# Up-projection of a gated MLP: seven products of half-size blocks in place of eight, with the inner features kept in DRAM

## The chip, the cores and the metric

The kernel runs on one core of a Trainium2 chip. The metric is the device time of one execution in microseconds, the median of three runs. TensorE is called PE here, VectorE DVE, ScalarE ACT, GpSimd POOL, and SyncE, which issues most of the loads, SP.

## What is computed

One decoder block on a sequence of 1024 tokens with 1024 features, in float32: attention of two kinds (stick-breaking and multi-head latent, MLA), an output projection, and a gated MLP with a causal convolution of width 3 over the tokens, all with RMSNorm and residuals. The part that matters here:

```
h = rms_norm(x, g_pre_ffn)
u = causal_depthwise_conv(h @ w_up, conv_w, conv_b)      # 1024 x 1024 times 1024 x 5632
gate, val = split(u, 2)                                  # 2816 features each
f = (gelu(gate, approximate=True) * val) @ w_down        # 2816 x 1024
x = x + rms_norm(f, g_post_ffn)
e = p @ w_ple
g = sigmoid(rms_norm(x, g_ple_gate) @ w_ple_gate + b_ple_gate)
x = x + rms_norm(g * e, g_post_ple)
```

## The kernel before, in words

Every matrix product is made from two float32r parts of each operand, a high and a low one (`split`, L90 to L97: ACT casts the high part, DVE or POOL subtracts to get the low part), and three of the four part products are added in PSUM. So one block of 128 x 128 weights times 512 tokens costs three matmuls with 512 columns, each of form 128*128 by 128x512.

Tokens go in two halves of 512 (`th` 0 and 1). After the attention the order is: output projection and norms of half 1 (`out_proj_sb`, `out_proj_mla`, L757 to L808), with the up-projection of half 0 (`ffn_up(0)`) filled in between; the rest of `ffn_up(0)`; `ffn_down(0)`; `ffn_up(1)`; `ffn_down(1)`; and the gate stage at the end.

`ffn_up` (L870) walks over 22 chunks `c` of 128 inner features. For a chunk it makes the gate's 128 rows (v=0) and the value's (v=1): 8 weight blocks times 3 matmuls for each, 48 matmuls in all (L895, L897, L901). The weights come through `split_w` (L107), 256 KB at a time, by the SP queue. The convolution reads PSUM: ACT multiplies by one tap and adds the bias (L913), DVE adds the other taps (L915, L917), and the two tokens at the seam between the halves go through the tile `halo` (L920 to L924). Gelu is ACT's (L938), the product with the value part DVE's (L939). The 22 feature tiles `f` stay in SBUF. `ffn_down` splits them and multiplies by `w_down` in 2 column halves x 22 chunks x 12 matmuls (L116 to L118).

What sets the order: the code is written as generators, and a `Fill` object steps the filler (here `ffn_up(0)`) by a credit at each yield of the main one; `WO_RATE` is the credit per yield of the output projection. A scheduler then orders the instructions of each engine by priority. Each engine runs its queue in that order, and so a waiting instruction holds all behind it. In `out_proj_mla(1)` a chain of steps ends the half: squares (L783), reciprocal roots (L125 to L135), scaling on DVE (L788), the residual's addition on POOL (L793), squares again, scaling (L800), and transposes on PE (L804), from which ACT and DVE make `h2`, the operand of the up-projection.

Of the kernel before, what the change touches and what calls it, by code (L numbers as in the profile page):

```python
# [38 lines left out]
WO_RATE = (1.0, 1.5)  # L39
AHEAD = 0.9  # L40
EMB_RATE = 1.0

LATER = (500, 0, 0, 2000)
# [6 lines left out]
def tile_hybrid_block(ctx: ExitStack, tc: tile.TileContext, a: dict, out: bass.AP):  # L50
# [13 lines left out]
    v_dram = dram.tile([P, NT, H], F32, name="v_dram")  # L64

# [213 lines left out]
    with tc.tile_pool(name="pre", bufs=1) as pre, \  # L279
# [27 lines left out]
        halo = const.tile([P, 2 * NCH, 2], F32, name="halo")  # L307
# [410 lines left out]
    def group_rstd(c0, ts):  # L718
# [3 lines left out]
        for j, t in enumerate(ts):  # L722
            src = o_tile(c0, t)
            sq = tmp().rearrange("p (c t) -> p c t", c=4)
            s_ = [sh.tile([P, P], dt, tag=f"s{i}", name=nm("s"))
                  for i, dt in enumerate((F32, F32R, F32R))]
            ps = bank()
            group_ssq(src, sq, s_, ps)
            dve.tensor_copy(ssm[:, j:j + 1], ps[:, 0:1])
            yield True  # L730
# [36 lines left out]
    def out_proj_mla(th, rows, h2):  # L767
# [8 lines left out]
        yield from group_product(4, ts, consume)  # L776
        hd_ = (slice(0, H), slice(H, D))
# [19 lines left out]
        for j in range(4):  # L797
            for k4, h_ in enumerate(hd_):
# [6 lines left out]
                d = [z[:, k4 * 4:k4 * 4 + 4, j * P:(j + 1) * P] for z in h2]  # L805
                split(d[0], d[1], ps.rearrange("p (k t) -> p k t", k=4))
                yield "chain"
# [33 lines left out]
    def embed_late():  # L841
        yield from embed(1, [sh.tile([P, H], F32R, tag=x, name=nm("pe"), bufs=b)
                             for x, b in (("y0", 1), ("y1", 1), ("raw", 1), ("t2", 6))])
# [12 lines left out]
    def f_tile(c):  # L856

        def two(p_, tag, bufs, first):
            if (c - first) % 2 == 0:
                f_tile.t = p_.tile([P, 2, H], F32, tag=tag, name=nm("f"), bufs=bufs)  # L860
            return f_tile.t[:, (c - first) % 2]

        if c < 8:
            return two(sh, "s4", 4, 0)
        if c < 14:
            return sh.tile([P, H], F32, tag="t2", name=nm("f"), bufs=6)
        if c < 18:
            return now["f"](c)
        return two(sh, "gb", 2, 18)

    def ffn_up(th, h2, f):
        nh, nl = h2
        todo = [(v * NCH + c, k4) for c in range(NCH) for v in range(2) for k4 in range(2)]
        ready = []

        def ahead(n):
            while len(ready) < n and todo:
                ci, k4 = todo.pop(0)
                ready.append(split_w(a["w_up"][ci, :, k4 * 4:k4 * 4 + 4, :], 512, None,
                                     now.get("light")))  # L880

        for c in range(NCH):
            ys = []
            while c >= 14 and "f" not in now or c >= 18 and "last" not in now:
                yield "wait"
            fc = f_tile(c)
            for v in range(2):
                ci = v * NCH + c
                ps = bank()
                for k4 in range(2):  # L890
                    ahead(3)
                    wh, wl = ready.pop(0)
                    for k in range(4):
                        kk = k4 * 4 + k
                        pe.matmul(ps, wh[:, k * P:(k + 1) * P], nh[:, kk], start=kk == 0,  # L895
                                  stop=False)
                        pe.matmul(ps, wh[:, k * P:(k + 1) * P], nl[:, kk], start=False, stop=False)  # L897
                    yield
                    for k in range(4):
                        kk = k4 * 4 + k  # L900
                        pe.matmul(ps, wl[:, k * P:(k + 1) * P], nh[:, kk], start=False,  # L901
                                  stop=kk == NK - 1)
                    if k4 == 0:
                        yield
                y = sh.tile([P, H], F32, tag=f"y{v}", name=nm("y"))
                if now.get("light"):
                    raw = sh.tile([P, H], F32, tag="raw", name=nm("raw"), bufs=1)
                    act.copy(raw, ps)
                    ps = raw
                    pool.tensor_scalar(y, ps, conv_w[:, ci, 2:3], conv_b[:, ci:ci + 1], ALU.mult,  # L910
                                       ALU.add)
                else:
                    act.activation(y, ps, AF.Identity, bias=conv_b[:, ci:ci + 1],  # L913
                                   scale=conv_w[:, ci, 2:3])
                dve.scalar_tensor_tensor(y[:, 1:], ps[:, :H - 1], conv_w[:, ci, 1:2], y[:, 1:],  # L915
                                         ALU.mult, ALU.add)
                dve.scalar_tensor_tensor(y[:, 2:], ps[:, :H - 2], conv_w[:, ci, 0:1], y[:, 2:],  # L917
                                         ALU.mult, ALU.add)
                if th == 0:
                    act.copy(halo[:, ci], ps[:, H - 2:])  # L920
                else:
                    dve.scalar_tensor_tensor(y[:, 0:1], halo[:, ci, 1:2], conv_w[:, ci, 1:2],
                                             y[:, 0:1], ALU.mult, ALU.add)
# [424 lines left out]
```

## Time and profile before

| | us |
|---|---|
| median of three runs | 1577.84 (1576.06 to 1579.86) |
| the profiled execution: its own time | 1584.88 |
| its span, from the first to the last instruction | 1583.1 |
| PE busy | 1479.8 |
| DVE busy | 1075.7 |
| ACT busy | 841.2 |
| POOL busy | 279.1 |

The profile has one execution. Groups of instructions are given by line, engine, operation and tile, with their number, busy time and mean duration; a second view gives busy time by stretches of the span; a third lists instructions in order of time. A matmul's duration overlaps with the next one's, since PE is pipelined: the distance from start to start is what one costs when PE never waits.

### The profile page before, as it was taken

How to read it: one execution, taken by the hardware profiler on the slowest of the kernel's cores; microseconds unless marked ns; L12 is line 12 of the kernel's file. 1: busy time of each engine (PE TensorE's matmuls, PEld its weight loads, DVE VectorE, ACT ScalarE, POOL GpSimd, SP SyncE). 2: the span in 40 equal slices, each digit the busy share in tenths (PEclk: the TensorE clock that was granted, in tenths of full speed). 3: DMA queues.
4: the chain of work that ended last, by engine and by line, in shares of the span. 5: the costliest groups of instructions: out<-in, count | busy, mean ns of one | idle time of the engine just before them, and what ended most of it. 6: DMA issues, size and time to landing. Idle time of an engine off the chain costs nothing. (4 is left out here: it accounts for less than half of the span.)

```text
span 1583.1 us, 20827 instructions
## 1 busy us (share of the span) xinstructions
PE 1479.8 (93%) x7032; PEld 1212.8 (77%) x7032; DVE 1075.7 (68%) x2021; ACT 841.2 (53%) x1649; POOL 279.1 (18%) x319
## 2 busy tenths in 40 slices
PE   4998998987899898899999999999999999999996
PEld 3977886865678676777888788888888888888875
DVE  4559477899777767866658855445976656444798
ACT  5356465677777675655544544444544444444542
POOL 7106300002243334241114000000000000000033
PEclk9999999999899899999999999999999999999998
DMA  6031310113444424234435532223432222233354
GB/s 197 22 100 41 106 35 14 47 53 126 143 139 148 130 90 157 67 110 145 150 117 191 169 103 88 99 93 99 152 122 94 93 94 96 92 95 97 127 178 168
DMA packets 109212, 173.78 MB, mean 110 GB/s; under 512 B 10913, under 2 KB 47681, under 8 KB 109105
## 3 DMA queue, kind: packets, MB, share of 16 engines
q1 hardware_dynamic: 100400, 142.71, 28.7%
q0 software_dynamic: 8704, 29.74, 5.1%
q8 instruction: 55, 0.90, 0.2%
q14 instruction: 53, 0.43, 0.1%
HBM read 142.26 MB, written 30.15 MB: 109 GB/s over the span
## 5 line engine op out<-in xcount | busy, mean ns | idle before, releaser
L94 DVE TENSOR_TENSOR wl<-ws,wh 128x512 fp32r<-128x512 f32 x281 | 203.9, 727 | 147.4 <-ACT wh L93 84.2
L93 ACT CAST wh<-ws 128x512 fp32r<-128x512 f32 x296 | 182.9, 620 | 219.6 <-PE mm L897 103.4
L897 PE MATMUL mm<-bh,wh 128*128 128x512 f32 x456 | 180.1, 395 | 0.0
L895 PE MATMUL mm<-bh,wh 128*128 128x512 f32 x456 | 180.1, 395 | 0.0
L94 DVE TENSOR_TENSOR fl<-f,fh 128x512 fp32r<-128x512 f32 x88 | 60.8, 692 | 117.9 <-PE mm L118 77.4
L94 DVE TENSOR_TENSOR tl<-tr,th 128x512 fp32r<-128x512 f32 x192 | 103.2, 550 | 45.3 <-ACT th L93 41.8
L901 PE MATMUL mm<-bh,wl 128*128 128x512 f32 x456 | 126.0, 396 | 0.0
L93 ACT CAST th<-tr 128x512 fp32r<-128x512 f32 x192 | 91.0, 485 | 59.6 <-PE tr L461 49.5
L93 ACT CAST fh<-f 128x512 fp32r<-128x512 f32 x88 | 54.6, 622 | 110.0 <-PE mm L117 84.4
L1166 POOL DMA_DIRECT2D x_dram<-fd x8 | 4.3, 538 | 616.9 <-DVE fd L1165 584.0
L461 PE MATMUL tr<-ident,w 128*128 128x128 f32 x576 | 102.6, 286 | 10.5 <-DVE tl L94 5.7
L895 PEld LDWEIGHTS mm<-bh,wh 128*128 128x128 f32 x456 | 85.9, 188 | 19.9
L897 PEld LDWEIGHTS mm<-bh,wh 128*128 128x128 f32 x456 | 85.9, 188 | 19.8
L901 PEld LDWEIGHTS mm<-bh,wl 128*128 128x128 f32 x456 | 85.6, 188 | 19.8
L649 DVE TENSOR_TENSOR_SCAN kc<-kc,one_f 128x128 f32<-128x128 f32 (+3 forms) x64 | 88.0, 1381 | 13.1 <-ACT kc L646 12.9
L116 PE MATMUL mm<-wh,fh 128*128 128x512 f32 x242 | 95.6, 396 | 0.0
L476 PE MATMUL av<-tl,v 128*128 128x512 f32 x192 | 77.2, 404 | 19.4 <-DVE tl L94 18.1
L117 PE MATMUL mm<-wl,fh 128*128 128x512 f32 x242 | 95.3, 394 | 0.0
L461 PEld LDWEIGHTS tr<-ident,w 128*128 128x128 f32 x576 | 73.9, 146 | 26.4 <-DVE tl L94 8.6
L475 PE MATMUL av<-th,v 128*128 128x512 f32 x192 | 78.5, 409 | 12.9 <-ACT th L93 7.6
L118 PE MATMUL mm<-wh,fl 128*128 128x512 f32 x242 | 82.5, 395 | 0.0
L116 PE MATMUL pj<-hTh,wh 128*128 128x512 f32 x160 | 65.6, 410 | 0.0
(425 smaller groups left out, 3808.2 us busy)
## 6 DMA issues: line engine op xcount, KB each, us to landing
ws<-in_w_up SPq DMA_DIRECT2D x176, 256.0 KB, 2.6
ws<-in_w_down SPq DMA_DIRECT2D x88, 256.0 KB, 2.6
ws<-in_w_o SPq DMA_DIRECT2D x32, 256.0 KB, 2.8
xl<-x_dram SPq DMA_DIRECT2D x16, 512.0 KB, 4.1
ws<-in_w_in SPq DMA_DIRECT2D x24, 256.0 KB, 2.9
t<-o_dram SPq DMA_DIRECT2D x24, 256.0 KB, 3.2
xl<-o_dram SPq DMA_DIRECT2D x24, 256.0 KB, 2.9
xt<-in_x SPq DMA_DIRECT2D x8, 512.0 KB, 6.0
```

The source lines that it names most:

```text
L93: act.copy(h, src)
L94: (pool if on_pool else dve).tensor_tensor(l, src, h, ALU.subtract)
L116: pe.matmul(ps, lh, rh, start=start, stop=False)
L117: pe.matmul(ps, lh, rl, start=False, stop=False)
L118: pe.matmul(ps, ll, rh, start=False, stop=stop)
L461: pe.transpose(tr[:, c:c + P], w[i][:, j * P:(j + 1) * P], ident)
L475: pe.matmul(av[:, lo:], v(j), th[:, lo:], start=j == 0, stop=False)
L476: pe.matmul(av[:, lo:], v(j), tl[:, lo:], start=False, stop=j == last)
L649: dve.tensor_tensor_scan(rev, rev, one_f[:, 0:1].to_broadcast([P, n]), 1.0, ALU.mult, ALU.mult)
L895: pe.matmul(ps, wh[:, k * P:(k + 1) * P], nh[:, kk], start=kk == 0, stop=False)
L897: pe.matmul(ps, wh[:, k * P:(k + 1) * P], nl[:, kk], start=False, stop=False)
L901: pe.matmul(ps, wl[:, k * P:(k + 1) * P], nh[:, kk], start=False, stop=kk == NK - 1)
```

## The change

With the weights of a chunk cut into four blocks (v = gate or value rows, k4 = first or second half of the 1024 input features) and the tokens' operand into four as well (feature half, token half), the product of the two 2 x 2 arrays of blocks is made by Winograd's form of Strassen's scheme: seven block products instead of eight, with four sums on the weights' side and four on the tokens' side. A block product is 12 matmuls of the same form as before.

- Two of the seven products need no sums: they take the gate's blocks and half 0 of the tokens. `up_first` makes them in place of `ffn_up(0)`, as filler, for all 22 chunks, and POOL writes the results to DRAM (`p1_dram`, `u_dram`).
- The tokens' sums `t1` to `t4` are made once, in `combined`, where the chain of the output projection of half 1 made `h2` before: per tile of 128 tokens 5 POOL operations with 128x512 elements, and on DVE 6 besides the scaling.
- The weights' sums are made for each chunk: four operations of 128x512 on POOL (`up_sums`, `up_sum_4`). Of the five splits of a chunk, POOL makes three low parts and DVE two.
- The other five products run after the output projection, in a stage of their own, both token halves together, 60 matmuls per chunk. DVE adds the first product and the partial sums out of PSUM, in five operations of 128x512, into tiles of 1024 tokens; the convolution then reads SBUF, in operations of 1024 elements; the halo is gone. The result goes to `f_dram` by a DMA that POOL issues.
- `ffn_down` reads the features back from DRAM: its loop loads 512 KB per 12 matmuls instead of 256 KB. The end of half 0 (`finish`) is filled into `ffn_down(1)`, it was in `ffn_up(1)`. The loads of the three broadcast rows of gains move ahead, into `ffn_down(0)`.
- `WO_RATE` goes from (1.0, 1.5) to (0.3, 2.5): now 0.3 for the products' yields and 2.5 for those of sums and chain.

```
+    def combined(j, b12, b22, first, ts_):
...
+        b11 = raw(0)
+        t1 = tmp()
+        dve.tensor_tensor(t1, b12, b11, ALU.subtract)
+        s22 = tmp()
+        act.copy(s22, b22)
+        t2 = tmp()
+        dve.tensor_tensor(t2, s22, t1, ALU.subtract)
+        t3 = tmp2()
+        dve.tensor_tensor(t3, s22, b12, ALU.subtract)
+        out("t1", t1, True)
+        yield "chain"
+        out("t3", t3)
+        b21 = raw(1)
+        t4 = tmp2()
+        pool.tensor_tensor(t4, b21, t2, ALU.subtract)
+        out("t2", t2)
+        out("b22", b22)
+        yield "chain"
+        out("t4", t4, True)
+        yield "chain"
...
+    def up_sums(raw, s):
+
+        a21, a22, a11 = (raw(1, 0), raw(1, 1), raw(0, 0))
+        pool.tensor_tensor(s[0], a21, a22, ALU.add)
+        pool.tensor_tensor(s[1], s[0], a11, ALU.subtract)
+        pool.tensor_tensor(s[2], a11, a21, ALU.subtract)
+        return (s[1], False), (s[0], False), (s[2], True), (a22, True)
+
+    def up_sum_4(raw, s1, dst):
+        pool.tensor_tensor(dst, raw(0, 1), s1, ALU.subtract)
+        return ((dst, True),)
...
+    def conv(v, c, u):
+        y = up_tile(f"y{v}", S, 2)
+        ci = v * NCH + c
+        act.activation(y, u, AF.Identity, bias=conv_b[:, ci:ci + 1], scale=conv_w[:, ci, 2:3])
+        for d in (1, 2):
+            dve.scalar_tensor_tensor(y[:, d:], u[:, :S - d], conv_w[:, ci, 2 - d:3 - d],
+                                     y[:, d:], ALU.mult, ALU.add)
+        return y
...
+        times(py_, "t2", True)
+        dve.tensor_tensor(q[0], p1, py_, ALU.add)
+        times(pz_, "t1", True)
+        times(py_, "t3")
+        dve.tensor_tensor(q[1], p1, py_, ALU.add)
+        dve.tensor_tensor(u[1][:, H:], q[1], pz_, ALU.add)
+        times(py_, "t4")
+        dve.tensor_tensor(u[1][:, :H], p1, py_, ALU.add)
+        times(pz_, "b22")
+        dve.tensor_tensor(u[0][:, H:], q[0], pz_, ALU.add)
+        y = [conv(v, c, u[v]) for v in range(2)]
+        act.activation(y[0], y[0], AF.Gelu_apprx_tanh)
+        dve.tensor_tensor(y[0], y[0], y[1], ALU.mult)
+        pool.dma_start(f_dram[c], y[0])
...
             for c in range(NCH):
-                wh, wl = split_w(a["w_down"][c * P:(c + 1) * P, ds_])
-                fh = fp.tile([P, H], F32R, tag="fh", name=nm("fh"), bufs=2)
-                fl = fp.tile([P, H], F32R, tag="fl", name=nm("fl"), bufs=2)
-                split(fh, fl, f[c])
+                w, fr = up_tile("wr", 512, WR), up_tile("wr", 512, WR)
+                sp.dma_start(w, a["w_down"][c * P:(c + 1) * P, ds_])
+                sp.dma_start(fr, f_dram[c][:, th * H:th * H + H])
```

How the order moves, at the places that count. First DVE in the up-projection, before: one value part and one gate part of `ffn_up(1)` (`mm` and `pj` are PSUM banks, `wl` the low part of a weight block, `y` the convolution's result).

```order
L94 TENSOR_TENSOR wl_11632<-ws_11629,wh_11631 128x512
L915 SCALAR_TENSOR_TENSOR y_11604<-pj_11534,c_conv_w,y_11604 128x511
L922 SCALAR_TENSOR_TENSOR y_11604<-halo,c_conv_w,y_11604 128x1
L917 SCALAR_TENSOR_TENSOR y_11604<-pj_11534,c_conv_w,y_11604 128x510
L924 SCALAR_TENSOR_TENSOR y_11604<-halo,c_conv_w,y_11604 128x2
L94 TENSOR_TENSOR wl_11659<-ws_11656,wh_11658 128x512
```

The same engine in the new stage, one chunk's worth of it (`ws` a weight's low part, `u` the sums out of PSUM with a bank `mm` or `pj` as one input, `q` the partial sums).

```order
L1217 SCALAR_TENSOR_TENSOR y_2363_9629<-u_2349_9531,c_conv_w,y_2363_9629 128x1023
L98 TENSOR_TENSOR ws_9039<-s_9722,ws_9038 128x512
L1241 TENSOR_TENSOR u_2367_9643<-q_2371_9648,pj_9646 128x512
L1217 SCALAR_TENSOR_TENSOR y_2363_9629<-u_2349_9531,c_conv_w,y_2363_9629 128x1022
L1237 TENSOR_TENSOR q_2387_9758<-p_2382_9751,mm_9756 128x512
L1248 TENSOR_TENSOR y_2363_9629<-y_2363_9629,y_2364_9633 128x1024
L1243 TENSOR_TENSOR u_2367_9643<-p_2365_9640,mm_9645 128x512
L98 TENSOR_TENSOR ws_9039<-s_9721,ws_9038 128x512
L1217 SCALAR_TENSOR_TENSOR y_2381_9744<-u_2367_9643,c_conv_w,y_2381_9744 128x1023
L1245 TENSOR_TENSOR u_2366_9642<-q_2370_9647,pj_9646 128x512
L1217 SCALAR_TENSOR_TENSOR y_2381_9744<-u_2367_9643,c_conv_w,y_2381_9744 128x1022
L1240 TENSOR_TENSOR q_2388_9759<-p_2382_9751,mm_9756 128x512
```

The convolution's DVE operations have become twice as long, with both inputs in SBUF, and five operations with one input in PSUM stand between them.

Second POOL in the same stage. Before, its queue from the end of the output projection to the end of the up-projections held five DMA issues and nothing else:

```order
L794 DMA x_dram<-row_7458 128x1024
L1166 DMA x_dram<-fd_9868 128x1024
L1166 DMA x_dram<-fd_9869 128x1024
L1166 DMA x_dram<-fd_9870 128x1024
L1166 DMA x_dram<-fd_9871 128x1024
```

Now it holds this for each of the chunks (`s` a sum of weight blocks, `wr` a loaded block, `ws` a low part):

```order
L928 TENSOR_TENSOR s_9832<-wr_9836,wr_9838 128x512
L98 TENSOR_TENSOR ws_9039<-s_9724,ws_9038 128x512
L929 TENSOR_TENSOR s_9833<-s_9832,wr_9840 128x512
L1249 DMA f_dram_119<-y_2363_9629 128x1024
L930 TENSOR_TENSOR s_9834<-wr_9840,wr_9836 128x512
L98 TENSOR_TENSOR ws_9039<-s_9723,ws_9038 128x512
L934 TENSOR_TENSOR s_9835<-wr_9845,s_9833 128x512
L98 TENSOR_TENSOR ws_9039<-wr_9838,ws_9038 128x512
```

Seven operations on 128x512 elements, all with two inputs in SBUF, and one DMA issue, which waits for DVE's last operation of a chunk (L1248), have moved onto POOL.

More of the change, by code (lines that the diff above doesn't have):

```diff
@@ new lines, in up_first @@
+    def up_first(h2):
+        todo = [(c, k4) for c in range(NCH) for k4 in range(2)]
+        ready = []
+        for c in range(NCH):
+            ps = now["up"]()
+            for k4 in range(2):
+                while len(ready) < 3 and todo:
+                    ready.append(split_w(up_block(0, todo[0][0], todo.pop(0)[1])))
+                b = [z[:, k4 * 4:k4 * 4 + 4] for z in h2]
+                yield from up_product(ps, ready.pop(0), b, k4 == 0)
+                t = sh.tile([P, H], F32, tag="uf", name=nm("uf"), bufs=3)
+                act.copy(t, ps)
+                pool.dma_start((p1_dram, u_dram)[k4][c], t)
+                yield True if k4 else None
@@ new lines, in tile_hybrid_block @@
+    with tc.tile_pool(name="wo", bufs=1, side="right", reuse_waits="tile") as wo_:
+        now["wo"] = wo_
+        rows1 = [sh.tile([P, D], F32, tag="s4", name=nm("row"), bufs=4) for _ in range(4)]
+        for r in out_proj_sb(1, rows1):
+            fill.step(WO_RATE[r in ("sums", "chain")])
+        for r in out_proj_mla(1, rows1, (h2[0], tb)):
+            fill.step(WO_RATE[r in ("sums", "chain")])
+        fill.drain()
+        slots = [big_a.tile([P, NK, H], F32R, tag="b", name=nm("ws")) for _ in range(2)]
+        ready = now["splits"](slots)
@@ L1219, in ffn_down @@
         return nt
[L1221 to L1228 removed]
+    nts = [ffn_down(th) for th in range(2)]
+    up_cm.__exit__(None, None, None)
     bg = bcast("b_ple_gate")
```

249 lines of the change are left out of this document (126 added, 123 removed).

## The prediction

> **What bounds the kernel now.** I read the page first, then busy time by stages, then instructions in order of time, and last the groups by line. The page says that PE is nearly always busy.
>
> ```profile
> span 1583.1 us, 20827 instructions
> PE 1479.8 (93%) x7032; PEld 1212.8 (77%) x7032; DVE 1075.7 (68%) x2021; ACT 841.2 (53%) x1649; POOL 279.1 (18%) x319
> ```
>
> The share is an average, so I cut the span where the change acts: output projection of half 1 with `ffn_up(0)` as filler (690 to 842), its chain (842 to 907), the rest of `ffn_up(0)`, `ffn_down(0)`, `ffn_up(1)` (1101 to 1349), `ffn_down(1)`, gate. Columns are the length, then busy time (and number) for PE, weight loads, DVE, ACT and POOL, then PE's granted clock, the DMA share and GB/s.
>
> ```profile
> 690.00:842.00 152.00, 150.96 (x656) 121.70 (x655) 96.10 (x161) 78.32 (x148) 32.50 (x26) 1.00 0.45 139
> 842.00:907.00 65.00, 64.09 (x292) 51.94 (x291) 58.81 (x98) 34.08 (x67) 15.79 (x12) 1.00 0.54 185
> 907.00:981.00 74.00, 74.00 (x320) 59.93 (x320) 42.26 (x61) 31.31 (x59) 0.00 (x0) 1.00 0.33 105
> 981.00:1101.00 120.00, 120.00 (x516) 96.45 (x515) 57.52 (x89) 52.75 (x88) 0.00 (x0) 1.00 0.29 96
> 1101.00:1349.00 248.00, 248.00 (x1086) 201.38 (x1085) 171.05 (x393) 115.56 (x182) 2.13 (x4) 1.00 0.33 109
> 1349.00:1473.00 124.00, 124.00 (x533) 99.61 (x532) 61.21 (x96) 55.71 (x91) 0.00 (x0) 1.00 0.30 94
> 1473.00:1583.00 110.00, 94.81 (x436) 76.35 (x434) 91.03 (x268) 44.11 (x89) 31.54 (x35) 0.96 0.48 163
> ```
>
> From 690 to 1473 us PE is busy without a gap worth the name, at full clock, and DVE, ACT and POOL have room. There a matmul less is time less, as long as the other engines keep up.
>
> **What a matmul costs.** Twelve matmuls of `ffn_up(1)` lie between the first and the last of these starts:
>
> ```profile
> 1105.29 0.40 PE L895 MATMUL mm<-bh,wh 128*128 128x512 f32 x1
> ...
> 1107.15 1.10 PE L901 MATMUL mm<-bh,wl 128*128 128x512 f32 x4
> 1108.09 0.40 PE L895 MATMUL mm<-bh,wh 128*128 128x512 f32 x1
> ```
>
> They take 2.80 us, so one costs 0.2333 us, not the 0.40 of its row, in which it overlaps its neighbours. By the rows' 0.40 the saving below would be 106 us, which I don't believe. The Trainium skill says the same (Trainium Kernel Development and Optimization, Performance Expectations): matmul busy time misleads because matmuls are pipelined.
>
> **Part 1: PE, -61.6 us.** 22 chunks x 8 matmuls of each 96 go: 44 x 48 = 2112 of the up-projection become 22 x 84 = 1848, 264 fewer, and the order of the changed kernel counts 6768 matmuls against 7032. 264 x 0.2333 = 61.6 us, nothing of it hidden, since PE is full there. The rest of PE's work is the same.
>
> **Part 2: the new stage, +22 us (0 to +95).** A chunk's five products are 60 matmuls, 14.0 us; that is the time in which the other engines must do theirs. Prices, from groups by line:
>
> ```profile
> L1164 DVE SCALAR_TENSOR_TENSOR fd<-fd,rn,g_post_ffn 128x1024 f32<-128x1024 f32 x8 | 10.2, 1280 | 0.1
> L1165 DVE TENSOR_TENSOR fd<-fd,xl 128x1024 f32<-128x1024 f32 x8 | 9.7, 1218 | 0.0
> L94 DVE TENSOR_TENSOR fl<-f,fh 128x512 fp32r<-128x512 f32 x88 | 60.8, 692 | 117.9 <-PE mm L118 77.4 <-PE av L118 26.8 <-ACT fh L93 12.1
> L1272 DVE TENSOR_TENSOR ge<-mm,b_ple_gate 128x512 f32<-128x512 f32 x10 | 6.8, 684 | 3.2 <-DMA out_dram<-ge 1.6 <-PE mm L118 1.5
> L1166 POOL DMA_DIRECT2D x_dram<-fd x8 | 4.3, 538 | 616.9 <-DVE fd L1165 584.0 <-issue 16.6 <-ACT bh L93 16.3
> L93 ACT CAST wh<-ws 128x512 fp32r<-128x512 f32 x296 | 182.9, 620 | 219.6 <-PE mm L897 103.4 <-PE pj L897 39.0 <-PE av L897 24.0
> L1145 ACT ACTIVATE junk<-fd 128x1024 bf16<-128x1024 f32 x16 | 16.9, 1056 | 18.2 <-DVE fd L1165 18.1
> ```
>
> DVE per chunk: 4 convolution steps x 1.28, the gate's product 1.22, 2 low parts x 0.69, 5 sums out of PSUM x 0.68: 11.1 us, of which 7.7 have both inputs in SBUF. ACT: 5 x 0.62 + 3 x 1.06 = 6.3 us, no matter. POOL: 7 x 1.29 (row below) + 0.54 = 9.6 us. Each fits into 14.0 alone. Together they don't quite, and the trace of before shows it, at the end of the output projection. DVE's rows in order of time stand first, then POOL's, then minimum, median and maximum in ns of the lines (of L788 the group's mean too):
>
> ```profile
> 853.12 6.94 DVE L788 SCALAR_TENSOR_TENSOR row<-row,rn,g_post_mix 128x1024 f32<-128x1024 f32 x4
> ...
> 861.68 0.74 DVE L915 SCALAR_TENSOR_TENSOR y<-mm,c_conv_w,y 128x511 f32<-128x511 f32 x1
> ...
> 864.04 4.36 DVE L94 TENSOR_TENSOR wl<-ws,wh 128x512 fp32r<-128x512 f32 x1
> ```
>
> ```profile
> 854.48 8.43 POOL L793 TENSOR_TENSOR row<-row,xl 128x512 f32<-128x512 f32 x4 [17.30 <-DVE row L788]
> ...
> 863.47 2.56 POOL L793 TENSOR_TENSOR row<-row,xl 128x512 f32<-128x512 f32 x2
> ```
>
> ```profile
> L788 DVE SCALAR_TENSOR_TENSOR row<-row,rn,g_post_mix x8: 1280/1940/2314, 601.7 to 857.7; 128x1024 f32<-128x1024 f32 x8
> ```
>
> ```profile
> L788 DVE SCALAR_TENSOR_TENSOR row<-row,rn,g_post_mix 128x1024 f32<-128x1024 f32 x8 | 14.3, 1829 | 0.0
> ```
>
> ```profile
> L793 POOL TENSOR_TENSOR row<-row,xl x8: 1300/1587/2276, 854.5 to 868.1; 128x512 f32<-128x512 f32 x8
> ```
>
> ```profile
> L745 POOL TENSOR_TENSOR xl<-xl,xl x16: 1285/1294/1829, 710.1 to 835.9; 128x512 fp32r<-128x512 f32 x16
> ```
>
> A DVE operation with two SBUF inputs that meets a POOL operation waits for it: 1.28 becomes 2.31, so POOL's holds it off for 1.03 us; POOL's becomes 2.28 when it is the one to wait. Once a low part of 0.69 took 4.36 while POOL ran one operation after the other. An operation that reads PSUM isn't touched: L915 at 861.68 kept its 0.74 while POOL was busy until 862.91.
>
> In the new stage 7 DVE operations of this kind and 7 of POOL's meet in every chunk. If they take turns, POOL's turn falls five times on a sum out of PSUM, which hides 0.68 of it, and twice between two neighbours: 5 x (1.03 - 0.68) + 2 x 1.03 = 3.8, so DVE needs 11.1 + 3.8 = 14.9 us. By the mean of L788, 1.83, 0.55 above its minimum with both queues full, 7 x 0.55 = 3.9 gives 15.0. I take 15.0: 22 x 1.0 = +22. The ends: nothing waits that PE doesn't cover (14.0, 0 us), and every meeting costs the whole 1.03 (11.1 + 7.2 = 18.3, +95 us).
>
> The Trainium skill (SBUF — State Buffer, Who interferes with whom) states the rule: a DVE instruction with two SBUF inputs contends with a GpSimd instruction that reads SBUF, and the second to issue is blocked until the first is through. The trace agrees on who is hit; for the length it shows 1.03 of 1.29 us.
>
> **Part 3: from the output projection to the new stage, +20 us (8 to 42).** The filler is half as long, and the chain must be done before the first product, which needs all four token tiles.
>
> ```profile
> L753 PE MATMUL pj<-wh,xl x16: 389/394/399, 735.1 to 842.0; 128*128 128x512 f32 x16
> ```
>
> ```profile
> L804 PE MATMUL tr<-ident,xl x32: 270/272/328, 882.8 to 906.7; 128*128 128x128 f32 x32
> ```
>
> Before, 40.8 us passed from the projection's last matmul (842.0) to the first transpose (882.8), all of it under filler. In the new order 135 filler matmuls stand there, 31.5 us; DVE was 90% busy in this stretch, much of it with the filler's convolution, which is gone, so I take a gap of 4 (0 to 9). Then POOL's sums: 23 operations and 6 DMA issues stand between the second tile's first sum and the last one (5 operations per tile, and four for the weights), 23 x 1.29 + 6 x 0.54 = 33 us, some 4 of them behind the last low part of `t1`. PE has 48 filler matmuls, 11.2 us, and 32 transposes, some 3 us by four in 0.35 us:
>
> ```profile
> 905.73 0.60 PE L804 MATMUL tr<-ident,xl 128*128 128x128 f32 x4
> 906.08 0.48 PE L901 MATMUL av<-bh,wl 128*128 128x512 f32 x1
> ```
>
> 29 - 14 = 15, and 1 for the lock: +16 (8, if more sums run early, to 33, if DVE's two-input work there, 24 operations of about 0.7, 17 us, comes between).
>
> **Part 4: the rest, +3 us (0 to 8).** `ffn_down` loads 512 KB in 2.8 us, 187 GB/s, where it loaded half.
>
> ```profile
> DMA  6031310113444424234435532223432222233354
> GB/s 197 22 100 41 106 35 14 47 53 126 143 139 148 130 90 157 67 110 145 150 117 191 169 103 88 99 93 99 152 122 94 93 94 96 92 95 97 127 178 168
> ws<-in_w_down SPq DMA_DIRECT2D x88, 256.0 KB, 2.6
> ```
>
> At 191 GB/s a slice of before has its DMA engines half busy, so it fits; a load lands in 2.6 us and five buffers give 7. Three broadcast rows, 1.5 MB, stand in the SP queue amid these loads: 8 us at that rate against the 7 covered. `finish` brings four tiles of 1.28 + 1.22 and some 3.5 us of smaller steps on DVE, 24 us as an estimate, into a stage where it had 61 of 124: hidden. The added writes (44 by `up_first`, 0.54 us each, on POOL) lie beside 160 us of PE's work. All added waits stay on their engine: POOL's DMA waits for L1248, and behind it are weights made more than a chunk ahead.
>
> **Sum.** -61.6 + 22 + 20 + 3 = -16.6 us. The profiled execution took 1584.9 (span 1583.1 and 1.8 around it), so 1568.3 in its terms; the median is 7.0 below it, 1561.2. I forecast 1561; less than 0.2%, 3 us, can't be told from no change here.
>
> **Rivals.**
> - The stage runs at PE's pace, 14.0 us a chunk, since the queues slide past each other: -38.6, 1539. For it: DVE 11.1 and POOL 9.6 both fit. Against it: 7.7 + 7 x 1.03 = 14.9 us of a lock that one at a time holds. Chance 0.22.
> - Slower: a POOL operation shuts DVE out for all of its 1.29 us and isn't covered by the sums out of PSUM, as in the 4.36 us above. 7.7 + 7 x 1.29 = 16.7 us per chunk, +59, total +21: 1599 (with POOL's DMA issue in the same queue 17.3 and 1612). It decides from 15.75 us a chunk, (61.6 - 23) / 22 above 14.0. Against it: no meeting of one with one cost over 1.03. Chance 0.22. This is what the skill's rule of the shared ports, read literally, would make of the kernel.
> - The chain, with 14 us of cover, is exposed for 45 instead of 20: +8, 1586. Chance 0.08.
> - `ffn_down` is late by 0.5 us in each of its 88 steps, from loads: +44 for 3, 1602. Chance 0.06.
> - That the matmuls aren't saved I leave out: the order has 264 fewer.
>
> The forecast itself keeps 0.42, with 1548 to 1574. **Range** 1532 to 1603: it takes in the first rival, the slower one at 16.7 and the two small ones. Faster 0.62 (forecast and first rival, less a little), within 0.2% 0.07, slower 0.31.
>
> **What would show it.** Right: new stage about 330 us long for 22 chunks, DVE over 95% busy in it, convolution steps (L1217) with a median above 1.28 and a maximum near 2.3, sums out of PSUM at 0.68; a gap of PE of some 20 us before the first product; `ffn_down` at 123 us per half. Wrong: a stage of 308 us with L1217 at 1.28 (the first rival), or one above 346 us (the second); PE waiting for `wr` loads in `ffn_down`.

## The result and the profile after

The changed kernel takes 1593.53 us (median of 4 runs, 1590.27 to 1598.62), against 1577.76 of the kernel before on the same chip: a ratio of 1.0103, with a 95% interval of 1.0088 to 1.0119. It is slower by 1%, where I had forecast faster by 1%; the time lies within the range of 1532 to 1603. The profiled execution took 1593.64 us, 8.7 more than the one before; the sum had come to -16.6, so 25 us of loss had been missed. The other 7 us between 1561 and 1593.5 come from the step to the median: the profiled execution of before was 7 us above its median, that of the changed kernel is at it.

The page of the changed kernel says that PE has the forecast 6768 matmuls, and that it is less busy:

```profile
span 1591.5 us, 20521 instructions
PE 1434.4 (90%) x6768; PEld 1169.9 (74%) x6768; DVE 1164.3 (73%) x1869; ACT 831.4 (52%) x1575; POOL 607.6 (38%) x548
```

Where the time of PE went shows when the same stretches are cut as before. Columns: length; busy time and number for PE, weight loads, DVE, ACT and POOL; PE's granted clock; DMA share; GB/s. The rows are the output projection of half 1 with its filler; from its last matmul to the tokens' first transposes; on to the first product of the new stage; its first 25 matmuls; the rest of the new stage; the two halves of `ffn_down`.

```profile
684.00:807.00 123.00, 120.28 (x521) 96.23 (x521) 51.29 (x96) 58.63 (x105) 33.08 (x42) 1.00 0.56 181
807.00:851.00 44.00, 34.21 (x125) 25.65 (x124) 30.90 (x46) 17.30 (x32) 24.53 (x24) 0.88 0.69 233
851.00:889.00 38.00, 20.84 (x81) 15.48 (x78) 33.11 (x30) 17.51 (x33) 28.54 (x26) 0.72 0.18 63
889.00:902.00 13.00, 8.11 (x25) 5.77 (x25) 5.16 (x5) 3.57 (x6) 9.52 (x7) 0.76 0.33 93
902.00:1238.00 336.00, 311.76 (x1316) 246.39 (x1317) 308.44 (x266) 136.54 (x177) 284.61 (x169) 0.99 0.43 139
1238.00:1360.00 122.00, 120.82 (x528) 98.81 (x528) 65.47 (x104) 57.51 (x94) 1.76 (x4) 1.00 0.68 223
1360.00:1482.00 122.00, 122.00 (x551) 100.31 (x550) 83.09 (x189) 64.73 (x112) 2.67 (x5) 1.00 0.63 203
```

The busy time misleads here, since at the lower clock of the second to fourth row a matmul's own time is longer (0.63 us instead of 0.40 from 860.5 to 863.5 us, for one); the count doesn't. At 0.2333 us each, and 2.8 us for 32 transposes, PE's work in the second row is 125 x 0.2333 = 29.2 of 44 us, in the third 14.2 of 38, in the fourth 5.8 of 13: 14.8 + 23.8 + 7.2 = 46 us lost between the projection and the new stage. In the stage itself it is 1316 x 0.2333 = 307 of 336: 29 lost. In `ffn_down` nothing is. With the 61.6 saved this makes +13; the part of the kernel ahead of the first row ended 5 us earlier (684.3, before 689.0), and the total is +8.7. The one profiled execution of before may have been late there already, which would be most of the 7 us above.

Of the signs that the forecast named for the stage, the convolution's steps have a median of 1722 ns above a minimum of 1268, and the sums out of PSUM keep their 0.68 us (671 to 690 ns in all five lines, one of which is shown). Others were missed: DVE is 92% busy, not over 95%, the longest step took 4.67 us instead of some 2.3, and the whole stage, 350 us, is longer than the 346 us that were to speak for the slower rival. Its row from 902 on, with 15.3 us a chunk, lies under the 15.75 at which that rival begins; what takes the whole over 346 is the start, 13 us for the first 25 matmuls.

```profile
L1217 DVE SCALAR_TENSOR_TENSOR y<-u,c_conv_w,y x88: 1268/1722/4666, 916.7 to 1245.0; 128x1023 f32<-128x1023 f32 x44, 128x1022 f32<-128x1022 f32 x44
L1243 DVE TENSOR_TENSOR u<-p,mm x15: 675/680/686, 914.7 to 1237.4; 128x512 f32<-128x512 f32 x15
```

In the transition two things stand out. The first, in order of time on POOL, SP's queue and ACT: POOL's last sum of the first weight blocks ends, then the filler's weight loads are issued, and ACT, which had waited 6.9 us for one of them, goes on.

```profile
815.56 1.27 POOL L930 TENSOR_TENSOR s<-ws,ws 128x512 f32<-128x512 f32 x1
...
817.69 1.78 SPq L108 DMA_DIRECT2D ws<-in_w_up  x3
...
821.78 0.62 ACT L97 CAST wh<-ws 128x512 fp32r<-128x512 f32 x1 [6.88 <-DMA ws<-in_w_up]
```

The sums' raw blocks sit in the three `ws` buffers into which the filler loads its own weights. The second, on DVE and then on POOL, while the third tile is combined: a DVE operation that takes 0.68 us alone takes 5.13, for as long as POOL has operations one behind the other.

```profile
876.59 0.69 DVE L843 TENSOR_TENSOR t<-t,tr 128x512 f32<-128x512 f32 x1 [3.40 <-ACT t L839]
877.19 5.13 DVE L841 TENSOR_TENSOR t<-t,t 128x512 f32<-128x512 f32 x1
```

```profile
876.82 1.28 POOL L934 TENSOR_TENSOR uf<-ws,s 128x512 f32<-128x512 f32 x1
878.08 1.25 POOL L98 TENSOR_TENSOR t4l<-t,t4h 128x512 fp32r<-128x512 f32 x1
879.30 1.25 POOL L832 TENSOR_TENSOR t<-bh,bh 128x512 f32<-128x512 f32 x1
880.52 1.25 POOL L98 TENSOR_TENSOR t1l<-t,t1h 128x512 fp32r<-128x512 f32 x1
```

It is the longest of several: in the 38 us ahead of the first product nine of DVE's thirty operations of 128x512 take 0.9 to 4.5 us more than the shortest of their kind, 16 us together.

For the fourth row, the first 25 matmuls, these are the longest waits between 889 and 902 us that lead to PE's (in total, times, longest): a cast for a load, and PE for that cast and for `t2`.

```profile
ACT ws L97 <- DMA wr<-in_w_up: 5.7, 1, 5.7
PE mm L915 <- ACT ws L97: 3.3, 1, 3.3
PE mm L915 <- ACT t2h L97: 1.5, 1, 1.5
```

### The profile page after: what moved, and what is told of

It is laid out like the page before. It is cut to its first block, busy times and chain, and to the rows that moved or that the text cites. A ratio compares the mean times of both kernels' runs of the same rounds, so it can differ in the third digit from the quotient of the medians.

```text
span 1591.5 us, 20521 instructions
## 1 busy us (share of the span) xinstructions
PE 1434.4 (90%) x6768; PEld 1169.9 (74%) x6768; DVE 1164.3 (73%) x1869; ACT 831.4 (52%) x1575; POOL 607.6 (38%) x548
## 5 line engine op out<-in xcount | busy, mean ns | idle before, releaser
L1217 DVE SCALAR_TENSOR_TENSOR y<-u,c_conv_w,y 128x1023 f32<-128x1023 f32 x88 | 162.8, 1852 | 9.3 <-ACT y L1215 9.2
L98 DVE TENSOR_TENSOR wl<-ws,wh 128x512 fp32r<-128x512 f32 x73 | 63.5, 879 | 70.1 <-ACT wh L97 33.2
L464 PE MATMUL tr<-ident,w 128*128 128x128 f32 x576 | 103.2, 287 | 10.1 <-DVE tl L98 6.0
L98 DVE TENSOR_TENSOR f<-wr,f 128x512 fp32r<-128x512 f32 x88 | 60.7, 690 | 68.5 <-PE pj L122 34.3
L1215 ACT ACTIVATE y<-u,c_conv_b,c_conv_w 128x1024 f32<-128x1024 f32 x44 | 54.8, 1245 | 89.7 <-DVE u L1245 53.1
L98 POOL TENSOR_TENSOR ws<-s,ws 128x512 fp32r<-128x512 f32 x42 | 88.9, 2121 | 3.0 <-ACT ws L97 3.0
L120 PE MATMUL mm<-wh,f 128*128 128x512 f32 x220 | 85.9, 393 | 0.0
L121 PE MATMUL mm<-wl,f 128*128 128x512 f32 x220 | 85.5, 391 | 0.0
L97 ACT CAST wh<-ws 128x512 fp32r<-128x512 f32 x76 | 46.7, 620 | 74.3 <-DMA ws<-in_w_up 27.8
L97 ACT CAST wh<-wr 128x512 fp32r<-128x512 f32 x88 | 54.6, 621 | 49.4 <-DMA wr<-in_w_down 35.7
L98 DVE TENSOR_TENSOR wl<-wr,wh 128x512 fp32r<-128x512 f32 x88 | 63.1, 717 | 19.1 <-ACT wh L97 19.0
L122 PE MATMUL mm<-wh,f 128*128 128x512 f32 x220 | 74.1, 393 | 0.0
```

What stands on the lines that cost most here:

```text
L97: act.copy(h, src)
L98: (pool if on_pool else dve).tensor_tensor(l, src, h, ALU.subtract)
L120: pe.matmul(ps, lh, rh, start=start, stop=False)
L121: pe.matmul(ps, lh, rl, start=False, stop=False)
L122: pe.matmul(ps, ll, rh, start=False, stop=stop)
L464: pe.transpose(tr[:, c:c + P], w[i][:, j * P:(j + 1) * P], ident)
```

## Experiments

My theory, A in the expectations: DVE and POOL hold each other off wherever both have two-input work, in the stage and in the tokens' chain, which is what lengthened the transition. The rivals to it are that the loss lies elsewhere, in loads, in the order, or in POOL being occupied as such; that the transition has too little cover; R, that the filler between projection and stage starves for load buffers; and that PE's lower clock stretches the chain. Each expectation says with numbers what its letters stand for. All edits are made to the changed kernel unless said otherwise. The runs differ by up to 4 us in the parts ahead of the projection's end, and the kernel before took 1576.6 to 1579.2 us beside them, so the table also gives the two lengths that matter: from the projection's last matmul to the first product of the new stage, and from there to the stage's last product.

| kernel | median us | ratio to before, 95% interval | to the first product, us | stage, us |
|---|---|---|---|---|
| changed | 1593.5 | 1.0103 (1.0088 to 1.0119) | 82.1 | 350.1 |
| e1_raw | 1571.2 | 0.9961 (0.9946 to 0.9976) | 80.2 | 324.3 |
| e2_memset | 1564.4 | 0.9922 (0.9902 to 0.9942) | 79.1 | 317.6 |
| e3_chain_dve | 1579.3 | 1.0023 (0.9999 to 1.0047) | 70.4 | 347.7 |
| e4_hold | 1602.4 | 1.0161 (1.0145 to 1.0178) | 102.3 | 356.8 |
| e5_ring | 1589.0 | 1.0072 (1.0046 to 1.0097) | 68.4 | 353.7 |
| e6_exact | 1576.5 | 0.9989 (0.9972 to 1.0006) | 64.5 | 346.6 |
| e7_lows | 1586.1 | 1.0034 (1.0006 to 1.0061) | 81.9 | 339.7 |
| e8_bare | 1610.1 | 1.0200 (1.0168 to 1.0232) | 62.3 | 346.4 |
| e9_both | 1563.8 | 0.9907 (0.9885 to 0.9928) | 64.5 | 334.3 |
| e10_two | 1574.5 | 0.9967 (0.9953 to 0.9981) | 65.7 | 347.1 |
| e11_warm | 1599.5 | 1.0134 (1.0110 to 1.0157) | 82.2 | 347.8 |

**The stage: what POOL's sums cost.** In e1_raw the four sums of weight blocks per chunk are left out, and raw blocks multiplied in their place, so what it computes isn't the block:

```
-            s = [up_tile("s", 512, 4) for _ in range(4)]
-            for src, on_pool in up_sums(raw, s) + up_sum_4(raw, s[1], s[3]):
+            a21, a22, a11, a12 = (raw(1, 0), raw(1, 1), raw(0, 0), raw(0, 1))
+            for src, on_pool in ((a11, False), (a21, False), (a21, True), (a22, True),
+                                 (a12, True)):
```

> The changed kernel without the four sums of weight blocks per chunk in the new stage: each product takes a raw block, so its output is not the block's. POOL keeps 3 low parts and one DMA issue per chunk. If DVE and POOL hold each other off in this stage (theory A), 4 of 7 meetings go and DVE needs 11.1 + 3 x 0.55 = 12.8 us a chunk, under PE's 14.0: the stage (336 us from 902 to 1238 in the changed kernel) falls to 308 to 314, and the total by some 24, to about 1570. If PE is held there by its own dependences on the sums out of PSUM or by loads (theory B), the stage stays over 328 and the total within 6 of 1593.

In e2_memset each sum is replaced by two memsets on POOL (the sums aren't computed either), which keep POOL occupied but read nothing:

```
+            for i in range(4):
+                for _ in range(2):
+                    pool.memset(s[i], 0.5)
```

> The changed kernel with each of the four weight sums of a chunk replaced by two POOL fills of the same tile, which write but read nothing: the weights are constants there and the output is not the block's. POOL is as busy as an order of magnitude (some 4 us a chunk of fills). If what holds DVE is that both engines read SBUF with two inputs (theory A), the fills don't hold it: stage 308 to 316, as without sums. If it is POOL's mere occupation or its queue order (theory B), the stage stays over 326.

Measured: 1571.2 and 1564.4. Theory A holds: with the memsets POOL is busy for 195 of 307 us, against 133 of 315 with no sums, and the stage runs as fast as without sums, or a little faster. With the sums POOL was busy for 285 of 336 us, so the memsets occupy it less; but they do so for most of the stage, and the convolution's median step is near its shortest again. First the stage's row of e1_raw, then that of e2_memset and its convolution steps (minimum, median and maximum):

```profile
901.00:1216.00 315.00, 303.67 (x1311) 245.41 (x1310) 262.60 (x260) 135.19 (x173) 132.65 (x86) 0.99 0.45 149
```

```profile
898.00:1205.00 307.00, 299.66 (x1304) 245.02 (x1304) 262.20 (x261) 135.47 (x174) 195.42 (x249) 0.99 0.46 153
L1222 DVE SCALAR_TENSOR_TENSOR y<-u,c_conv_w,y x88: 1270/1284/2845, 916.4 to 1213.8; 128x1023 f32<-128x1023 f32 x44, 128x1022 f32<-128x1022 f32 x44
```

By 60 matmuls a chunk, 1304 in 307 us are 14.1 us a chunk, nearly PE's own pace of 14.0, and the changed kernel's 1316 in 336 are 15.3. The median step is back at 1284 ns, although POOL still makes its three low parts, with two inputs in SBUF each. The Trainium skill (SBUF — State Buffer, Who interferes with whom) says that a two-input DVE instruction contends with a GpSimd instruction that reads SBUF and not with one that only writes it; e2_memset agrees.

**The tokens' chain without POOL.** In e3_chain_dve the raw blocks, `t4` and the low parts of `t1` and `t4` leave POOL for DVE. The first half's blocks are taken from their high part alone, so they lack the low part:

```
-        b11 = raw(0)
+        b11, b21 = [first[0][:, i * 4:i * 4 + 4, j * P:(j + 1) * P] for i in range(2)]
...
-        out("t1", t1, True)
+        out("t1", t1)
...
-        pool.tensor_tensor(t4, b21, t2, ALU.subtract)
+        dve.tensor_tensor(t4.rearrange("p (k t) -> p k t", k=4), b21,
+                          t2.rearrange("p (k t) -> p k t", k=4), ALU.subtract)
```

> The changed kernel with POOL taken out of the tokens' sums: t1 to t4 and all their low parts on DVE, and the first half's blocks are taken from the high part alone, so the output is a little off. From the first transpose (851) to the first product of the new stage (892) 41 us pass in the changed kernel. Theory A, that DVE and POOL holding each other off stretched this: DVE alone needs about 7.7 us per tile, the stretch falls to 31 to 34 and the total by 8, to about 1585. Theory C, that the order of ACT's queue and a slower PE clock stretch it: the stretch stays at 40 or more, and the total within 3.

Measured: 1579.3, 14 less. The way to the first product is 12 us shorter although DVE has 12 operations more, and from the first transpose on it takes 26 us instead of 38. In the last 38 us only three DVE operations are still stretched, by 3 us together instead of 16. That fits theory A, larger than I thought. But the edit takes 20 operations out of POOL's queue, and eight of them, the additions of the raw blocks, nobody makes any more: how much came from the lock and how much from POOL's queue getting shorter, this run can't part.

**More filler in the transition.** In e4_hold the filler is held back in the projection, so that more of it is left for the chain:

```
-WO_RATE = (0.3, 2.5)
+WO_RATE = (0.0, 0.5, 2.5)
-            fill.step(WO_RATE[r in ("sums", "chain")])
+            fill.step(WO_RATE[{"sums": 1, "chain": 2}.get(r, 0)])
```

> The changed kernel with the filler held back: WO_RATE 0 at the yields of the projection's products, 0.5 at those of the sums, 2.5 at those of the chain, so that in its order 324 filler matmuls instead of 171 stand behind the projection's last matmul. Theory C2, that the transition lacks cover: the projection (684 to 806) shortens to some 90 us, the chain keeps its 86, PE is kept busy and at full clock, and the first product comes at 860 instead of 892: total 1563 (1555 to 1575). Rival D, that the projection itself is bound by its loads and by ACT and POOL: it keeps over 115 us, and the total is 1590 to 1600.

Measured: 1602.4, slower, and outside both expectations. The rows are the projection and the way to the first product:

```profile
684.00:786.00 102.00, 86.13 (x343) 65.48 (x342) 41.78 (x81) 42.50 (x75) 25.18 (x27) 0.93 0.44 140
786.00:888.00 102.00, 84.90 (x356) 65.08 (x354) 76.77 (x94) 48.99 (x88) 62.92 (x60) 0.97 0.54 186
```

The second stretch now has 324 matmuls of 0.2333 us and the transposes, 78 of 102 us, so it loses 24 instead of 39. But the projection has lost its cover and loses 102 - 80 = 22 instead of 2, and 132 of the filler's matmuls came to stand between the last transposes and the first product, where nothing needs cover. So the cover as such wasn't tested; what it shows is that the same filler can't cover both places.

**The load buffers.** In e5_ring the first sums' raw blocks get buffers that are free at that time (those of the output projection's weights):

```
-            if (v, k4) != (1, 1):
-                return load_w(up_block(v, 0, k4))
-            w = kept()
+            w = kept() if (v, k4) == (1, 1) else now["wo"].tile(
+                [P, 512], F32, tag="wh", name=nm("t"), bufs=4)
```

> The first weight sums' three raw blocks no longer take the three load buffers of the filler's weights (ring `ws`), but free buffers of their own; nothing else changes. Theory R (the filler starves: its next weight block waits 6.9 us for a buffer that POOL's sums hold, ACT waits for that block, and the tokens' steps queue behind on ACT): the stretch from the projection's last matmul (807) to the first transpose (851) shrinks by about 7 us, total 1586. Theory A (POOL and DVE hold each other there) or the DMA rate of 230 GB/s: within 3 us of 1593.5.

Measured: 1589.0, 4.5 less by the medians, and 9 by the profiled spans (the profiled execution was the fastest of six). The first transposes come 33 us behind the projection instead of 44, and the first product 13.7 us earlier: theory R, for more than I gave it. ACT's waits for the filler's weights in this stretch fall from 12.8 to 5.6 us. Part of the 11 us is work that moved: 100 of the filler's matmuls stand in these 33 us, where 125 stood in the 44. So the loss there falls from 14.8 to 33 - 100 x 0.2333 = 9.7 us, and the rest of the gain lies behind the first transposes. Some 3 us of it are handed back in the stage's first chunk, as the last of these rows shows: 16 us instead of 13 for the first 24 or 25 matmuls. The first row is the way to the first transposes, the second the whole way to the first product.

```profile
807.00:840.00 33.00, 25.62 (x100) 19.96 (x99) 26.16 (x43) 13.61 (x24) 24.54 (x22) 0.90 0.68 236
807.00:876.00 69.00, 49.26 (x205) 37.86 (x203) 60.82 (x75) 33.41 (x61) 53.69 (x49) 0.90 0.49 170
876.00:892.00 16.00, 8.07 (x24) 5.86 (x25) 5.96 (x5) 3.09 (x5) 9.85 (x8) 0.77 0.30 96
```

**Both.** e6_exact is e5_ring with POOL out of the chain as in e3_chain_dve, but with both parts of the first half subtracted:

```
+        dve.tensor_tensor(r4(t1), r4(b12), b11[0], ALU.subtract)
+        dve.tensor_tensor(r4(t1), r4(t1), b11[1], ALU.subtract)
...
+        dve.tensor_tensor(r4(t4), b21[0], r4(t2), ALU.subtract)
+        dve.tensor_tensor(r4(t4), r4(t4), b21[1], ALU.add)
```

> Both at once: POOL taken out of the tokens' sums (raw sums and low parts of t1 and t4 done on DVE, three DVE operations of 0.68 us more per tile than in the earlier run of that kind, since both parts of the first half are subtracted), and the buffers of e5_ring. Theory A: the earlier run's 14 us are kept less some 4 x 1 us for the added operations, so 1583, and with the 7 us of theory R 1576. If the two theories name the same microseconds (a chain that waits for one is let wait for the other), 1582 to 1584.

Measured: 1576.5, as for two separate losses. The lengths say the same: way and stage together are 14.1 us shorter in e3_chain_dve than in the changed kernel, 10.1 in e5_ring and 21.1 here, with eight DVE operations of 0.68 us more than in e3_chain_dve (two per tile, where the expectation says three). The way to the first product is 64.5 us, with 42.5 us of PE's work in it: 22 lost.

```profile
811.00:875.00 64.00, 46.58 (x203) 36.26 (x201) 56.95 (x90) 33.72 (x61) 33.43 (x33) 0.91 0.53 186
```

**Low parts of the stage on DVE.** In e7_lows POOL keeps the four sums and gives its three low parts away:

```
             for src, on_pool in up_sums(raw, s) + up_sum_4(raw, s[1], s[3]):
-                yield up_split(src, on_pool)
+                yield up_split(src, False)
```

> In the new stage the three low parts of weights that POOL makes go to DVE: POOL 4 two-input operations per chunk instead of 7, DVE 3 x 0.69 more. By the turn-taking sum (prediction, part 2): DVE 13.2, POOL's four turns fall on the five sums out of PSUM at 0.35 each, 14.6 us per chunk where 15.3 was measured: -15, 1578. By a DVE that is the bound and pays a fixed price per meeting (four POOL operations fewer were worth 26 us, so three are worth 20, against 3 x 0.69 x 22 = 45 us added): +25, 1618.

Measured: 1586.1, 7 less: the direction of the turn-taking sum, at two thirds of its size in the stage.

```profile
902.00:1229.00 327.00, 309.50 (x1322) 248.51 (x1323) 313.08 (x328) 138.59 (x178) 156.11 (x103) 0.99 0.42 142
L1217 DVE SCALAR_TENSOR_TENSOR y<-u,c_conv_w,y x88: 1266/1276/2352, 921.8 to 1236.1; 128x1023 f32<-128x1023 f32 x44, 128x1022 f32<-128x1022 f32 x44
```

The convolution's steps now run at 1276 ns, and 1322 matmuls in 327 us are 14.8 us a chunk, where the sum said 14.6. DVE is 96% busy; it does more work in less time, since three operations of 0.69 us cost less than the meetings that they had on POOL (the three together: e10_two below gains nothing with two of them).

**The chain bare.** In e8_bare nearly all of the filler goes ahead of the projection's end:

```
-WO_RATE = (0.3, 2.5)
+WO_RATE = (0.3, 6.0)
```

> 156 of the filler's 171 matmuls move from behind the projection's last matmul to ahead of it, so the tokens' chain runs bare. PE's 36 us for them are then paid in the projection, where PE has no gap. If the chain's length (82 us from the projection's last matmul to the first product) is its own on DVE, POOL and ACT, the first product comes at about 915 and the total is about 26 us longer, 1620. If the filler stretches the chain (its casts and copies ahead of the chain's in ACT's queue, its loads ahead of x's, its products ahead of the transposes at half the clock), the chain takes about 55 us and the total is within 5 us of 1593.5.

Measured: 1610.1, between the two. The projection grew by 41 us, the chain shrank by 20:

```profile
684.00:848.00 164.00, 159.56 (x695) 127.90 (x694) 57.20 (x110) 74.50 (x132) 40.19 (x55) 1.00 0.55 180
848.00:910.00 62.00, 12.52 (x48) 8.41 (x47) 49.05 (x63) 21.10 (x38) 50.93 (x38) 0.56 0.25 93
```

Bare, the chain takes 62 us; the filler around it stretched it to 82. With the buffers and the POOL edit it takes 64.5 with all of the filler inside, so neither a length of its own of 82 us nor the filler as such was the cause.

**Together, and a variant.** e9_both is e6_exact with the edit of e7_lows.

> The two edits that cut different stretches, together: POOL out of the tokens' sums with the load buffers set apart (a run of 1576.5, first product at 875 instead of 889), and the stage's three low parts on DVE (a run of 1586.1, stage 340 us instead of 350). If the losses before the stage and in it are separate, their gains add: 1593.5 - 17 - 7.5 = 1569, faster than before. If the shorter transition only moves work into the stage, 1576 and no better than the first edit alone.

Measured: 1563.8, 5 below the 1569 of the two gains added, a ratio of 0.9907 (0.9885 to 0.9928): faster than the changed kernel and than the kernel before. The rows are the way to the first product, the first 24 matmuls and the rest of the stage:

```profile
808.00:872.00 64.00, 46.23 (x201) 35.95 (x200) 56.86 (x91) 34.04 (x61) 33.36 (x33) 0.91 0.53 185
872.00:881.00 9.00, 7.99 (x24) 5.69 (x24) 6.18 (x9) 2.88 (x5) 3.56 (x3) 0.70 0.68 226
881.00:1206.00 325.00, 306.57 (x1321) 246.03 (x1321) 314.06 (x327) 138.49 (x178) 156.48 (x103) 1.00 0.42 140
```

Against the changed kernel the first product comes 17 us earlier (872.0 for 889.0) and the stage is 16 shorter, 4 of them up to its 25th matmul: the two losses add. e10_two leaves one of the three low parts, that of `a22`, on POOL:

```
-                yield up_split(src, False)
+                yield up_split(src, on_pool and src is not s[2] and src is not s[3])
```

> As e9_both, but only two of the three low parts go to DVE and one stays on POOL. With all three DVE was busy for 98% of the stage's middle, with none 94% and POOL 91%. If what counts is DVE's own busy time, one operation of 0.69 us less per chunk gives up to 15 us: 1554 to 1565. If a POOL operation costs DVE about as much in meetings as its own 0.69 us, it is a draw: within 4 us of e9_both.

Measured: 1574.5, 11 slower than e9_both, which neither reading expected. PE waited 29 us for high parts of weights where it had waited 9.5. First the waits of e9_both between 900 and 1210 us (in total, times, longest), then those of e10_two, then e10_two's POOL operation:

```profile
PE mm L918 <- ACT ws L97: 9.5, 6, 1.8
```

```profile
PE mm L918 <- ACT ws L97: 20.5, 12, 2.0
PE av L918 <- ACT ws L97: 8.6, 5, 1.7
```

```profile
L98 POOL TENSOR_TENSOR ws<-wr,ws 128x512 fp32r<-128x512 f32 x17 | 38.8, 2284 | 0.0
```

The one operation takes 2.28 us instead of 1.29. From its 25th matmul on the stage takes 337.5 us, as in e6_exact with all three low parts on POOL (337.6), and 325.2 in e9_both: moving two of them gains nothing, and the third 12 us. Why the weights come later with one on POOL than with none, I haven't shown; that stays open.

**PE's clock.** In e11_warm PE transposes every token tile four more times, into a bank that nobody reads:

```
+                if th == 1:
+                    warm = one_bank(pav, "av")
+                    for k in list(range(4)) * 4:
+                        pe.transpose(warm[:, k * P:(k + 1) * P], n[:, k * P:(k + 1) * P], ident)
```

> The changed kernel with 16 more transposes behind each tile half's four, into a PSUM bank that nobody reads: 128 in all, some 11 us of PE at 0.0875 us each, where PE waits for some 39 us and its granted clock is at 0.5 to 0.75. They leave every result as it is. If the low clock stretches the tokens' chain (a filler product took 5.1 us there instead of 2.8, and ACT waited 6.5 us for it), keeping PE busy brings the first product forward, from 889 to about 883, total 1588. If the low clock only follows from the waiting and costs nothing, the first product stays at 889 or comes up to 11 us later, total 1593 to 1605.

Measured: 1599.5, and 82.2 us to the first product, as before. Three stretches of the chain in the changed kernel, then the same in e11_warm; the third number from the right is the granted clock:

```profile
860.00:868.00 8.00, 5.63 (x20) 4.13 (x20) 8.00 (x9) 4.29 (x8) 6.00 (x5) 0.75 0.13 48
868.00:876.00 8.00, 5.82 (x16) 4.42 (x16) 5.19 (x5) 1.65 (x4) 4.38 (x5) 0.61 0.18 66
876.00:884.00 8.00, 0.96 (x4) 0.72 (x4) 7.41 (x4) 2.70 (x6) 7.28 (x7) 0.60 0.19 66
```

```profile
860.00:868.00 8.00, 5.33 (x38) 4.61 (x37) 6.80 (x7) 3.08 (x6) 5.52 (x4) 1.00 0.00 0
868.00:876.00 8.00, 5.70 (x40) 4.84 (x39) 8.00 (x8) 2.83 (x5) 4.96 (x7) 1.00 0.18 66
876.00:884.00 8.00, 7.94 (x60) 7.08 (x58) 7.89 (x7) 4.96 (x10) 7.98 (x7) 1.00 0.18 68
```

At the full clock the chain is as long, but that doesn't settle what the low clock costs. ACT's longest wait for a filler product fell from 6.54 to 3.34 us, and against that one of DVE's low parts was held for longer than any in the changed kernel, while POOL ran six operations and two DMA issues. ACT's wait in the changed kernel stands first, then in e11_warm, then that low part:

```profile
873.63 0.62 ACT L97 CAST wh<-s 128x512 fp32r<-128x512 f32 x1 [6.54 <-PE mm L917]
```

```profile
874.44 0.62 ACT L97 CAST wh<-s 128x512 fp32r<-128x512 f32 x1 [3.34 <-PE mm L921]
881.12 9.18 DVE L98 TENSOR_TENSOR t2l<-t,t2h 128x512 fp32r<-128x512 f32 x1
```

The steps of the last tile queue behind it, and the first product waits for them. So a gain from the clock can have been taken back by the longer hold; whether there was one stays open.

## Why the prediction was wrong

- **Part 1** was right: 264 matmuls fewer, at 0.2333 us each.
- **Part 2** was right in its mechanism and near in size, from the 25th matmul on: 15.3 us a chunk for 15.0, so +29 for +22. With the four sums replaced by writes the stage runs at 14.1 (e2_memset), so what keeps it from PE's pace, the first rival's, is the sums' reading. The slower rival's 16.7 us a chunk didn't come.
- **Part 3** is the step that failed: +46 for +20, beyond its upper end of 42. Its first term, "so I take a gap of 4", was 14.8. I had argued that DVE's queue would be shorter without the filler's convolution, and had not looked at what the filler needs: its weights share three buffers with the first sums' raw blocks, and ACT, which runs in order, held the tokens' steps behind a cast that waited 6.9 us for a load. In e5_ring, with buffers of their own, this term is 9.7: the load buffers account for 5 of the 11 us that I missed, and the other 6 stay open (in the chain behind, which then holds 25 matmuls more, the loss falls as well, from 23.8 to 15.4). The second term, +16, was 23.8: I had counted POOL's own queue and 1 us for the lock, and the lock stretched nine DVE operations by 16 us together, one of them to 5.13 us. e3_chain_dve gives 12 us back, but it takes POOL's queue out of the chain together with the lock; for the lock speaks that DVE's stretching fell from 16 to 3 us. The third loss, 7 us in the first 25 matmuls, I had not named at all. In the trace PE waits there 1.5 us for the high part of `t2` and 3.3 for a weight's cast, which itself waited 5.7 us for a load; in e9_both the 25th matmul comes 9 us behind the first instead of 13. With both edits the way to the first product loses 22 us in e6_exact. That this is near the 20 forecast is chance: 16 of the 20 stood for POOL's queue, which that run hasn't got in its chain.
- **Part 4** was right to its lower end: `ffn_down` lost nothing, at 203 to 223 GB/s.
- Of the rivals, the small one (the chain exposed for 45 instead of 20 us, chance 0.08) is what happened, with 46: its sum is +8.4 by the profiled execution, and +8.7 was measured (its 1586 misses the median by the 7 us of that step). That the sums agree to 0.3 us is luck: the stage lost 29 instead of 22, `ffn_down` 0 instead of 3, and 5 us were gained ahead of the projection. Nor was all of the 46 lost in the chain: 14.8 lie ahead of the first transposes, and 7.2 behind the first product. I had given it too little: I knew from the trace of before that a low part had once taken 4.36 us behind POOL's queue, and counted the lock in the stage at length but in the chain as 1 us, though there one operation waits for the other and no other work covers it.

## What to carry to other kernels

Before moving work to POOL, list DVE's operations with two SBUF inputs that run at that time: in a full stage such a neighbour took a chunk from 14.1 to 15.3 us, and in a serial chain, where nothing hides it, an operation of 0.68 us took 5.13, and once 9.18. A new early load that borrows an existing buffer ring takes it from whoever uses the ring as cover; ask which in-order queue then stands behind the starved load. A saving of PE's time is only as good as the seam in front of the shortened stage: here mending the way into the stage and the stage's queues brought the first product 17 us forward and made the stage 16 us shorter, more than half of the 61.6 that PE was spared.

## What the runs showed of the hardware

- Several POOL operations in a row can hold one DVE operation for all of them (5.13 us with four, 9.18 with six in e11_warm), while in e7_lows no step of the convolution took more than 2.35, 1.1 above its minimum.
- POOL's memsets into SBUF, eight per chunk, left the convolution's median at 1284 ns, where sums in their place had made it 1722; the three low parts on POOL were there in both.
- PE's granted clock fell to 0.60 in 8 us stretches while it waited, a filler product's matmuls started 0.43 us apart there instead of 0.233, and 128 idle transposes brought the clock to 1.00; the first product came no earlier by it. The Trainium skill (TensorE: Matmul & The Clock Gate, Part 1) says that an idle PE is clocked at half rate. The trace agrees: from 883 to 889 us, where the changed kernel's PE made eight transposes and waited, the granted clock was 0.50.
